# A chunked recurrence between projections: more buffers for a unit's tiles, and its score products in another pair of PSUM banks

## Chip, core and metric

One NeuronCore of a Trainium2 chip runs the whole kernel. The metric is the device time of one execution in microseconds (us). TensorE is called PE, its weight loads PEld, VectorE DVE, ScalarE ACT, GpSimd POOL and SyncE, which issues every DMA here, SP. Each engine works through its own list of instructions in the order in which they stand, and semaphores make it wait for the others.

## What is computed

Two decoder layers over 1024 tokens of 1024 channels in float32. Layer 0 mixes the tokens with a gated linear recurrence (HGRN2), layer 1 with latent attention; a causal conv gated MLP follows each. The change touches layer 0's mixer alone:

```python
q, f, i, g = jnp.split(h @ w_in, 4, axis=-1)        # 8 heads of 128
forget = lb + (1.0 - lb) * jax.nn.sigmoid(f)
key_in = 1.0 - forget
log_f = jnp.log(forget)
# per head, S_t = diag(exp(log_f_t)) S_{t-1} + k_t v_t^T ; o_t = S_t^T q_t, in chunks
o = _chunk_gated_recurrence(heads(jax.nn.silu(q)), heads(key_in), heads(i), heads(log_f))
o = _rmsnorm(o, out_norm) * jax.nn.silu(heads(g))
return o.reshape(B, S, D_MODEL) @ w_out
```

## The kernel before

Tokens are cut into two halves of 512 (`hf`), channels into 8 tiles of 128. Matrix products are made of three products of float32r parts (`hi*hi`, `hi*lo`, `lo*hi`), so that every weight tile from DRAM (`wraw`) is split into `whi` (a cast on ACT) and `wlo` (a subtraction, line 131, on POOL in the recurrence and on DVE in the output projection).

The recurrence works through 16 **units**, one for each head and half. A unit has two parts.

- `project` (lines 347 to 396): 48 matmuls of 512 columns for the forget gate and the query, into two PSUM banks with the tag `mm`, then 96 matmuls of 256 columns for value and gate, into the same two banks in turn. DVE, ACT and POOL make of them the tiles `Fg`, `K`, `q`, `Q`, `v` and `g`.
- `recur` (lines 398 to 473): the diagonal products `scores(q)`, 8 small matmuls, then six levels m = 1, 2, 4, 8, 16, 32. At each level PE makes `scores(Q)` (8 small matmuls, line 406), DVE writes them under a mask into `SD` (line 429), DVE multiplies half of `Q` by the decay of the blocks (line 417), and POOL half of `K` (line 419). The next level needs both. Then come a last product of 4 matmuls (`sc64`, line 432), the copies into `ST` on ACT (lines 436 to 438), the transposes of `K` (line 443) and their copy back on ACT (line 445), and for each of four chunks `po` (lines 451 and 453) and the update of the state, `pu` (line 456) and line 461. Then the squares of `po` on ACT (line 465), a reciprocal square root in small DVE instructions, and the scaling of `g` (line 471).

`flip` (line 475 on) transposes a unit's `g` on PE into the one `misc` bank and splits it, and `put_out` writes both parts to DRAM (`o_spill`). `out_projection` (line 309) reads all heads of a half back (`oall`), and makes 8 groups of 24 matmuls of 512 columns, each added to `x` on DVE (line 303).

The program is written as: recurrence of unit i, then projection of unit i+1, then flip of unit i. That is not the order in which it runs. The framework's scheduler fixes a list for each engine before the run; it may put an instruction earlier wherever the buffers and banks that it needs come free, and it puts the projection's matmuls between the steps of the recurrence.

So the buffers set how far a unit may run into the one before. Before the change a unit's `K`, `Q`, `v` and `Fg` have two buffers each, `SD` and `ST` one, and the block decays `tot1` to `tot32` one each. PSUM has eight banks: `mm` two, `misc` one, `wo` two, `sc` two, `o` one. All scores, `sc64`, the transposes `pT` and the four `pu` share the two `sc` banks; the two `wo` banks are used by the first projection only, and by later parts of the kernel.

Of the kernel before, what the change touches and what calls it, by code (L numbers as in the profile page):

```python
# [9 lines left out]
F32 = mybir.dt.float32  # L10
# [9 lines left out]
P = 128  # L20
D = 1024
S = 1024
HF = 512
# [7 lines left out]
LEVELS = (1, 2, 4, 8, 16, 32)  # L31
# [27 lines left out]
def trunk_kernel(ctx: ExitStack, tc: tile.TileContext, x, pos, par, gout, cst, msk, w_hin, w_hout,  # L59
# [9 lines left out]
    psg = ctx.enter_context(tc.tile_pool(name="psg", bufs=2, space=PSUM))  # L69

    def ps_mm():
        return psg.tile([P, HF], F32, tag="mm", name="ps_mm")
# [68 lines left out]
    def v3(ap, a):  # L141
        return ap.rearrange("p (a b) -> p a b", a=a)

    def acc3(ps, steps):
        n = len(steps)
        for i, (lh, ll, rh, rl) in enumerate(steps):
            pe.matmul(ps, lhsT=lh, rhs=rh, start=(i == 0), stop=False)  # L147
            pe.matmul(ps, lhsT=lh, rhs=rl, start=False, stop=False)  # L148
            pe.matmul(ps, lhsT=ll, rhs=rh, start=False, stop=(i == n - 1))  # L149
# [171 lines left out]
    def hgrn(layer, h):  # L321
        with ExitStack() as st:
            tp = st.enter_context(tc.tile_pool(name="g_t", bufs=2))
            early = st.enter_context(tc.tile_pool(name="g_e", bufs=2))
            wv = st.enter_context(tc.tile_pool(name="g_wv", bufs=1))
            ps = st.enter_context(tc.tile_pool(name="g_ps", bufs=1, space=PSUM))
# [24 lines left out]
            def project(hd, hf, bank=ps_mm):  # L351
                wf, wq, vgh, vgl = wts[hd]
                hh, hl, rb, y = h[hf]

                def proj(w):
                    p = bank()
                    acc3(p, [(w[0][:, k * P:(k + 1) * P], w[1][:, k * P:(k + 1) * P], hh[:, k, :], hl[:, k, :])
                             for k in range(KD)])
                    return p

                pf = proj(wf)
                Fg = early.tile([P, HF], F32, tag="F", name="Fg")
                K = tp.tile([P, HF], F32, tag="K", name="K")
                dve.tensor_tensor(out=Fg, in0=pf, in1=rb, op=ALU.mult)
                act.activation(out=K, in_=Fg, func=AF.Sigmoid, scale=-1.0)
                act.activation(out=Fg, in_=Fg, func=AF.Sigmoid)
                pool.tensor_scalar(out=Fg, in0=Fg, scalar1=oml[:, hd:hd + 1], scalar2=lb[:, hd:hd + 1],
                                   op0=ALU.mult, op1=ALU.add)
                pool.tensor_scalar(out=K, in0=K, scalar1=oml[:, hd:hd + 1], scalar2=0.0, op0=ALU.mult, op1=ALU.add)
                pq = proj(wq)  # L370
                q = early.tile([P, HF], F32, tag="q", name="q", bufs=1)
                Q = tp.tile([P, HF], F32, tag="Q", name="Q")
                dve.tensor_tensor(out=q, in0=pq, in1=rb, op=ALU.mult)  # L373
                act.activation(out=Q, in_=q, func=AF.Sigmoid)
                dve.tensor_tensor(out=q, in0=q, in1=Q, op=ALU.mult)
                dve.tensor_tensor(out=Q, in0=q, in1=Fg, op=ALU.mult)

                v = tp.tile([P, 4, P], F32, tag="v", name="v")
                g = tp.tile([P, 4, P], F32, tag="g", name="g", bufs=3)
                for tt in range(2):  # L380
                    pv = ps_mm()
                    for t2 in range(2):
                        t = 2 * tt + t2
                        ts_ = slice(t * P, (t + 1) * P)
                        acc3(pv[:, t2 * 256:(t2 + 1) * 256],
                             [(hh[:, k, ts_], hl[:, k, ts_], vgh[:, k, :], vgl[:, k, :]) for k in range(KD)])
                    p3 = v3(pv, 2)
                    for t2 in range(2):
                        t = 2 * tt + t2
                        yt = y[:, t:t + 1]  # L390
                        act.activation(out=v[:, t, :], in_=p3[:, t2, 0:P], func=AF.Identity, scale=yt)
                        act.activation(out=g[:, t, :], in_=p3[:, t2, P:2 * P], func=AF.Sigmoid, scale=yt)
                        dve.scalar_tensor_tensor(out=g[:, t, :], in0=p3[:, t2, P:2 * P], scalar=yt, in1=g[:, t, :],  # L393
                                                 op0=ALU.mult, op1=ALU.mult)
                pool.tensor_tensor(out=g, in0=g, in1=goutb[:, None, :].broadcast_to([P, 4, P]), op=ALU.mult)
                return Fg, K, q, Q, v, g

            def recur(hd, hf, prj, state):
                Fg, K, q, Q, v, g = prj

                def scores(qq):
                    sc = ps.tile([P, 4, 64], F32, tag="sc", name="sc", bufs=2)
                    for c in range(4):
                        for b in range(2):
                            sl = slice(c * P + b * 64, c * P + b * 64 + 64)
                            pe.matmul(sc[b * 64:b * 64 + 64, c, :], lhsT=K[:, sl], rhs=qq[:, sl], start=True, stop=True)  # L406
                    return sc

                SD = tp.tile([P, 4, 64], F32, tag="SD", name="SD", bufs=1)
                dve.tensor_tensor(out=SD, in0=scores(q), in1=fold[:, None, 0:64].broadcast_to([P, 4, 64]), op=ALU.mult)  # L410

                def scale(tot, m):
                    nb = HF // (2 * m)
                    tv = tot.rearrange("p (b two) -> p b two", two=2)
                    Qv = Q.rearrange("p (b two m) -> p b two m", two=2, m=m)
                    Kv = K.rearrange("p (b two m) -> p b two m", two=2, m=m)
                    dve.tensor_tensor(out=Qv[:, :, 1, :], in0=Qv[:, :, 1, :],  # L417
                                      in1=tv[:, :, 0:1].broadcast_to([P, nb, m]), op=ALU.mult)
                    pool.tensor_tensor(out=Kv[:, :, 0, :], in0=Kv[:, :, 0, :],
                                       in1=tv[:, :, 1:2].broadcast_to([P, nb, m]), op=ALU.mult)  # L420
                    nt = tp.tile([P, nb], F32, tag=f"tot{m}", name=f"tot{m}", bufs=2 if m == 64 else 1)
                    dve.tensor_tensor(out=nt, in0=tv[:, :, 0], in1=tv[:, :, 1], op=ALU.mult)
                    return nt

                tot = Fg
                for li, m in enumerate(LEVELS):
                    sc = scores(Q)
                    tot = scale(tot, m)
                    dve.copy_predicated(SD, masks[:, li, None, :].broadcast_to([P, 4, 64]), sc)
                sc = ps.tile([P, 4, 64], F32, tag="sc", name="sc64", bufs=2)  # L430
                for c in range(4):
                    pe.matmul(sc[0:64, c, :], lhsT=K[:, c * P:c * P + 64], rhs=Q[:, c * P + 64:(c + 1) * P],
                              start=True, stop=True)
                ST = tp.tile([P, 4, P], F32, tag="ST", name="ST", bufs=1)
                pool.memset(ST[64:P, :, 0:64], 0.0)
                act.copy(out=ST[0:64, :, 0:64], in_=SD[0:64])
                act.copy(out=ST[64:P, :, 64:P], in_=SD[64:P])
                act.copy(out=ST[0:64, :, 64:P], in_=sc[0:64])
                tot = scale(tot, 64)

                pT = ps.tile([P, 4, P], F32, tag="sc", name="pT", bufs=2)
# [7 lines left out]
                for c in range(4):  # L449
                    first = state is None  # L450
                    pe.matmul(po[:, c, :], lhsT=ST[:, c, :], rhs=v[:, c, :], start=True, stop=first)
                    if not first:
# [40 lines left out]
            goutb = wv.tile([P, P], F32, tag="goutb", name="goutb")  # L493
            nc.sync.dma_start(out=goutb, in_=gout.partition_broadcast(P))
            nc.sync.dma_start(out=cs, in_=cst)
            mstage = tp.tile([P, len(LEVELS), 64], F32, tag="ST", name="mstage", bufs=1)
            nc.sync.dma_start(out=mstage, in_=msk)
            dve.tensor_copy(out=masks, in_=mstage)
            prj = project(0, 0, ps_wo)
            h.append(norm_x(1, "mix", layer))  # L500
            states = {}
            for i, (hd, hf) in enumerate(units):
                if i:
                    put_out(*pend[:2], flip(pend[2]))
                g, states[hd] = recur(hd, hf, prj, states.get(hd))
                pend = (hd, hf, g)
                if i + 1 < len(units):
                    if units[i + 1][0] != hd:
                        weights(units[i + 1][0])
                    prj = project(*units[i + 1])  # L510
# [456 lines left out]

    h = [norm_x(0, "mix", 0)]
    h = hgrn(0, h)
    h = ffn(0, h)  # L970
    h = mla(h)
# [77 lines left out]
```

## Time and profile before

| what | value |
|---|---|
| median of 3 runs | 2585.41 us (2581.57 to 2588.17) |
| the profiled execution | 2581.05 us |
| its span, first to last instruction | 2579.2 us |
| PE busy in the span | 2483.0 us (96%) |
| DVE, ACT, POOL busy | 1698.1, 1080.6, 392.5 us |
| mean granted clock of PE | 0.987 of full speed |
| first and last score product of the recurrence | 46.5 and 615.7 us |

The span counts from the first instruction. "Idle" of an engine in a list of waits is the time in which none of its instructions ran, put down to what came last before it went on. Matmuls are pipelined: a bar of 0.28 us stands for a matmul that may be followed by the next after 0.12 us. A float32 matmul shows as two records.

### The profile page before, as it was taken

The numbers are of one execution on the slowest core, as the hardware profiler recorded it, in microseconds if no ns is written. First come the engines' busy times: TensorE is split into PE (matmuls) and PEld (weight loads), VectorE is DVE, ScalarE is ACT, GpSimd is POOL, SyncE is SP. The second block draws the span as 40 slices with busy tenths as digits, with TensorE's granted clock in tenths as the row PEclk, the third lists the DMA queues.
The fourth block names the chain that finished last, engine by engine and source line by source line (L and its number), as shares of the span: only waits on it lengthen the run. The fifth ranks groups of instructions, "written<-read, shape, count | busy, mean of one in ns | idle before, by whom it ended". The sixth has DMA issues, their size and how long they took to land.

```text
span 2579.2 us, 35799 instructions
## 1 busy us (share of the span) xinstructions
PE 2483.0 (96%) x13860; PEld 2069.2 (80%) x13860; DVE 1698.1 (66%) x3033; ACT 1080.6 (42%) x1777; POOL 392.5 (15%) x386
## 2 busy tenths in 40 slices
PE   7999999998999999999999999999999999999999
PEld 6888888876777778888888788888877787888887
DVE  8355555555788888774535777777578888875333
ACT  5322223322444444433433566656444444443322
POOL 3334445521100000000003323221000000000000
PEclk9999999999999999999999999989999999999999
DMA  3111111343433332264331000002543333226443
GB/s 138 42 50 50 50 50 66 113 144 121 154 120 111 108 112 89 90 230 155 128 126 50 17 34 33 34 26 103 200 155 120 109 110 111 91 91 220 155 170 116
DMA packets 88298, 270.18 MB, mean 105 GB/s; under 512 B 9920, under 2 KB 10304, under 8 KB 86976
## 3 DMA queue, kind: packets, MB, share of 16 engines
q1 hardware_dynamic: 88128, 267.90, 29.5%
q8 instruction: 109, 1.79, 0.3%
q14 instruction: 61, 0.50, 0.1%
HBM read 207.04 MB, written 60.82 MB: 104 GB/s over the span
## 4 chain that ended last, share of the span: by engine, by line
PE 86%; DVE 6%; ACT 3%; DMA 3%; issue 1%; SPq 0%; ACTq 0%; DVEq 0%
PE ps_mm L251 19%; PE ps_up L251 9%; PE ps_mm L147 8%; PE ps_mm L149 8%; PE ps_mm L148 7%; PE ps_up L942 7%; PE ps_mm L942 5%; PE ps_wo L942 5%; PE ps_wo L251 3%; PE sp L710 3%; PE ps_misc L942 2%; PE sc L406 2%; PE ps_misc L167 2%; DMA open_spill<-part 1%; PE ps_wo L739 1%
## 5 line engine op out<-in xcount | busy, mean ns | idle before, releaser
L128 ACT CAST whi<-wraw 128x1024 fp32r<-128x1024 f32 (+1 forms) x328 | 321.3, 993 | 579.2 <-PE ps_misc L942 236.6
L131 DVE TENSOR_TENSOR wlo<-wraw,whi 128x1024 fp32r<-128x1024 f32 (+1 forms) x298 | 337.9, 1146 | 286.3 <-ACT whi L128 285.9
L251 PE MATMUL ps_mm<-bop,whi 128*128 128x512 f32 x1536 | 477.7, 393 | 17.3 <-ACT x L888 9.5
L251 PEld LDWEIGHTS ps_mm<-bop,whi 128*128 128x128 f32 x1536 | 285.9, 188 | 89.8 <-ACT x L888 15.4
L251 PE MATMUL ps_mm<-bop,wlo 128*128 128x512 f32 x768 | 296.4, 391 | 0.9 <-DVE wlo L131 0.9
L862 DVE SCALAR_TENSOR_TENSOR x<-x,prm,x 128x1023 f32<-128x1023 f32 (+1 forms) x176 | 223.5, 1279 | 48.9 <-ACT x L859 47.9
L251 PE MATMUL ps_up<-bop,whi 128*128 128x512 f32 x704 | 220.7, 394 | 0.9 <-ACT whi L128 0.9
L251 PEld LDWEIGHTS ps_mm<-bop,wlo 128*128 128x128 f32 x768 | 144.2, 188 | 33.6 <-DVE wlo L131 2.2
L942 PE MATMUL ps_up<-ring,whi 128*128 128x512 f32 x528 | 159.9, 389 | 0.0
L251 PEld LDWEIGHTS ps_up<-bop,whi 128*128 128x128 f32 x704 | 131.8, 188 | 33.1 <-ACT whi L128 2.6
L417 DVE TENSOR_TENSOR Q<-Q,tot 128x256 f32<-128x256 f32 x96 | 65.6, 683 | 133.2 <-PE sc L406 105.3
L147 PE MATMUL ps_mm<-vgh,hh 128*128 128x256 f32 x512 | 146.0, 285 | 5.9 <-DVE q L373 5.6
L149 PE MATMUL ps_mm<-vgh,hl 128*128 128x256 f32 x512 | 145.4, 284 | 0.0
L148 PE MATMUL ps_mm<-vgl,hh 128*128 128x256 f32 x512 | 143.8, 281 | 0.0
L859 ACT ACTIVATE x<-x,prm 128x1024 f32<-128x1024 f32 x88 | 109.3, 1243 | 70.0 <-DVE x L886 48.2
L251 PE MATMUL ps_up<-bop,wlo 128*128 128x512 f32 x352 | 138.5, 394 | 0.0
L845 DVE TENSOR_TENSOR wraw<-wraw 128x512 f32<-128x512 f32 x176 | 120.8, 686 | 2.2
L147 PE MATMUL ps_mm<-hh,whi 128*128 128x512 f32 x288 | 115.7, 402 | 2.2 <-DVE g L393 1.2
L710 PE MATMUL sp<-kk,qq 128*128 128x256 f32 (+4 forms) x480 | 109.1, 363 | 8.7 <-ACT pp L725 8.5
L942 PEld LDWEIGHTS ps_up<-ring,whi 128*128 128x128 f32 x528 | 99.2, 188 | 20.7
L149 PE MATMUL ps_mm<-hh,wlo 128*128 128x512 f32 x288 | 115.5, 401 | 0.0
L888 ACT COPY x<-ps_mm 128x512 f32<-128x512 f32 x84 | 49.1, 584 | 153.0 <-PE ps_mm L251 153.0
(296 smaller groups left out, 5544.3 us busy)
## 6 DMA issues: line engine op xcount, KB each, us to landing
wraw<-in_w_up_dram SPq DMA_DIRECT2D x104, 512.0 KB, 3.7
wraw<-in_w_down_dram SPq DMA_DIRECT2D x88, 512.0 KB, 3.5
act_spill<-x SPq DMA_DIRECT2D x44, 512.0 KB, 2.6
araw<-act_spill SPq DMA_DIRECT2D x88, 256.0 KB, 3.6
wraw<-in_w_hin_dram SPq DMA_DIRECT2D x38, 512.0 KB, 3.5
oall<-o_spill SPq DMA_DIRECT2D x64, 256.0 KB, 4.6
o_spill<-oh SPq DMA_DIRECT2D x32, 256.0 KB, 2.0
o_spill<-ol SPq DMA_DIRECT2D x32, 256.0 KB, 2.2
```

What stands on the lines that cost most here:

```text
L128: act.copy(out=hi, in_=src)
L131: lo_eng.tensor_tensor(out=lo, in0=src, in1=hi.bitcast(F32), op=ALU.subtract)
L147: pe.matmul(ps, lhsT=lh, rhs=rh, start=(i == 0), stop=False)
L148: pe.matmul(ps, lhsT=lh, rhs=rl, start=False, stop=False)
L149: pe.matmul(ps, lhsT=ll, rhs=rh, start=False, stop=(i == n - 1))
L251: pe.matmul(p, lhsT=a[l][:, ks], rhs=b[:, r, k, :], start=first and k == 0 and n == 0, stop=k == KH - 1 and n == 2, skip_group_check=not f ...
L417: dve.tensor_tensor(out=Qv[:, :, 1, :], in0=Qv[:, :, 1, :], in1=tv[:, :, 0:1].broadcast_to([P, nb, m]), op=ALU.mult)
L710: pe.matmul(sp[:, 0:n], lhsT=qq[:, a, qs], rhs=kk[:, c, cl], start=(i == 0), stop=last)
L845: dve.tensor_tensor(out=o, in0=p, in1=q, op=op)
L859: act.activation(out=y, in_=u, func=AF.Identity, scale=cw(2, ff), bias=pcol("cb", layer * 44 + ff))
L862: dve.scalar_tensor_tensor(out=y[:, i:S], in0=u[:, 0:S - i], scalar=cw(2 - i, ff), in1=y[:, i:S], op0=ALU.mult, op1=ALU.add)
L942: pe.matmul(acc[d], lhsT=w[l][:, d * P:(d + 1) * P], rhs=a[:, r], start=j == 0 and n == 0, stop=j == NFF - 1 and n == 2)
```

## The change

`Fg`, `K`, `Q` and `v` get three buffers, `SD`, `ST` (with `mstage`, which shares its tag) and every `tot` two. The seven groups of score products of a unit, `scores(...)`, move from the pool's `sc` tag to the `wo` tag, two whole banks; `sc64`, `pT` and `pu` keep the two `sc` banks. No instruction is added or removed.

```diff
-                Fg = early.tile([P, HF], F32, tag="F", name="Fg")
-                K = tp.tile([P, HF], F32, tag="K", name="K")
+                Fg = early.tile([P, HF], F32, tag="F", name="Fg", bufs=3)
+                K = tp.tile([P, HF], F32, tag="K", name="K", bufs=3)
...
-                Q = tp.tile([P, HF], F32, tag="Q", name="Q")
+                Q = tp.tile([P, HF], F32, tag="Q", name="Q", bufs=3)
...
-                v = tp.tile([P, 4, P], F32, tag="v", name="v")
+                v = tp.tile([P, 4, P], F32, tag="v", name="v", bufs=3)
...
-                    sc = ps.tile([P, 4, 64], F32, tag="sc", name="sc", bufs=2)
+                    sc = psg.tile([P, 4, 64], F32, tag="wo", name="sc", padded_shape=[P, 8, 64])
...
-                SD = tp.tile([P, 4, 64], F32, tag="SD", name="SD", bufs=1)
+                SD = tp.tile([P, 4, 64], F32, tag="SD", name="SD", bufs=2)
...
-                    nt = tp.tile([P, nb], F32, tag=f"tot{m}", name=f"tot{m}", bufs=2 if m == 64 else 1)
+                    nt = tp.tile([P, nb], F32, tag=f"tot{m}", name=f"tot{m}", bufs=2)
...
-                ST = tp.tile([P, 4, P], F32, tag="ST", name="ST", bufs=1)
+                ST = tp.tile([P, 4, P], F32, tag="ST", name="ST", bufs=2)
```

The scheduler makes other lists of it. Three places follow; a number behind a name tells one tile from another of its kind.

**The end of a unit on PE**, in the middle of the recurrence: the unit whose tiles are `Q_1790`, `K_1758` and `v_1795`, and the next, `Q_2140` and `K_2108`. Before:

```order
L432 MATMUL sc64_2014<-Q_1790,K_1758 64x64 x4
L451 MATMUL po_2034<-v_1795,ST_2019 128x128 x2
L443 MATMUL pT_2028<-ident_85,K_1758 128x128 x4
L456 MATMUL pu_2038<-v_1795,K_1758 128x128
L456 MATMUL pu_2044<-v_1795,K_1758 128x128
L453 MATMUL po_2034<-state_2040,Q_1790 128x128
L451 MATMUL po_2034<-v_1795,ST_2019 128x128
```

Of the change, from the last of 10 value-and-gate matmuls that now stand behind `sc64_2014`:

```order
L149 MATMUL ps_mm_2202<-vgh_1722,hl_409 128x256
L406 MATMUL sc_2270<-q_2139,K_2108 64x64 x8
L406 MATMUL sc_2280<-Q_2140,K_2108 64x64
L451 MATMUL po_2034<-v_1795,ST_2019 128x128
L443 MATMUL pT_2028<-ident_85,K_1758 128x128 x4
L451 MATMUL po_2034<-v_1795,ST_2019 128x128
L406 MATMUL sc_2280<-Q_2140,K_2108 64x64 x7
L147 MATMUL ps_mm_2451<-hh_111,whi_2431 128x512
L148 MATMUL ps_mm_2451<-hl_112,whi_2431 128x512
```

Before, the last product, `po`, the transposes and the `pu` follow each other with nothing between. Now 10 matmuls and the next unit's first 9 score matmuls stand ahead of `po`, and 25 matmuls of 512 columns between the transposes and `pu_2038`. In units of the other half, the next unit's first score groups and 8 matmuls of 512 columns stand ahead of `po`, and 10 with a score group ahead of `pu`.

**POOL's list** over the levels of two units, where it has to split the next head's query weights (`wlo_2438`). Before:

```order
L419 TENSOR_TENSOR K_1389<-K_1389,tot2_1586 128x64x4
L395 TENSOR_TENSOR g_1796<-g_1796,goutb_226 128x512
L419 TENSOR_TENSOR K_1389<-K_1389,tot4_1600 128x32x8
L131 TENSOR_TENSOR wlo_2438<-wraw_2435,whi_2437 128x1024
L419 TENSOR_TENSOR K_1389<-K_1389,tot8_1614 128x16x16
```

Of the change:

```order
L419 TENSOR_TENSOR K_1758<-K_1758,tot1_1941 128x128x2
L131 TENSOR_TENSOR wlo_2438<-wraw_2435,whi_2437 128x1024
L369 TENSOR_SCALAR K_2108<-K_2108,lb4_200 128x512
L367 TENSOR_SCALAR Fg_2107<-Fg_2107,lb4_200,lb3_199 128x512
L435 MEMSET ST_2369 64x4x64
L419 TENSOR_TENSOR K_1758<-K_1758,tot2_1955 128x64x4
```

The split stands now between the levels 1 and 2 of a unit, with the gate work of the next projection right behind it.

**The end of the recurrence on PE**: the last matmul of the last unit (`po_6023`) and its flip (`ps_misc_6068`). Before:

```order
L453 MATMUL po_6023<-state_6042,Q_5779 128x128
L478 MATMUL ps_misc_6068<-ident_85,g_5785 128x128 x4
L167 MATMUL ps_misc_6377<-ones_90,acc_6354 128x2 x4
L147 MATMUL ps_mm_6447<-oall_6423,whi_6443 128x512
```

Of the change, from the last two of 27 output-projection matmuls that follow that `po_6023`:

```order
L148 MATMUL ps_mm_6479<-oall_6424,whi_6475 128x512
L149 MATMUL ps_mm_6479<-oall_6423,wlo_6476 128x512
L478 MATMUL ps_misc_6068<-ident_85,g_5785 128x128 x4
L167 MATMUL ps_misc_6377<-ones_90,acc_6354 128x2 x4
L147 MATMUL ps_mm_6447<-oall_6423,whi_6443 128x512
L147 MATMUL ps_mm_6479<-oall_6423,whi_6475 128x512
```

27 matmuls have moved into the place where nothing stood; flip, token sums and the rest of the two groups follow as before. The flip of the last head of the first half, which stood inside the first group of the first output projection, now stands inside the projection ahead of it.

## Rows read from the trace of the kernel before

**Rows 1.** Busy time by stretch (us, PE, PEld, DVE, ACT, POOL, clock, DMA share, GB/s).

```profile
150.00:545.00 395.00, 375.19 (x3419) 325.39 (x3418) 216.58 (x580) 118.38 (x322) 167.69 (x156) 1.00 0.19 65
545.00:660.00 115.00, 101.52 (x587) 80.19 (x586) 63.55 (x128) 33.67 (x59) 24.48 (x20) 0.94 0.38 129
```

**Rows 2.** PE's waits, 150 to 545 us: total, times, longest.

```profile
PE pu L456 <- ACT K L445: 8.8, 12, 0.7
PE ps_mm L147 <- DVE q L373: 5.4, 12, 0.7
PE po L451 <- ACT ST L438: 3.6, 8, 0.5
PE po L453 <- DVE state L461: 1.1, 5, 0.2
```

**Rows 3.** PE's waits, 545 to 660 us, the four longest.

```profile
PE ps_misc L478 <- DVE g L471: 4.5, 1, 4.5
PE ps_mm L147 <- DMA oall<-o_spill: 4.3, 2, 2.2
PE ps_misc L167 <- DVE ol L131: 1.4, 1, 1.4
PE ps_mm L147 <- DVE x L303: 1.2, 1, 1.2
```

**Rows 4.** PE in order of time at one unit's end: start, duration, instruction, idle before.

```profile
357.71 0.28 PE L148 MATMUL ps_mm<-vgl,hh 128*128 128x256 f32 x1
357.83 0.28 PE L149 MATMUL ps_mm<-vgh,hl 128*128 128x256 f32 x1
358.03 0.68 PE L432 MATMUL sc<-Q,K 128*64 128x64 f32 x8
359.17 0.71 PE L451 MATMUL po<-v,ST 128*128 128x128 f32 x4 [0.46 <-ACT ST L438]
...
361.09 0.71 PE L456 MATMUL pu<-v,K 128*128 128x128 f32 x4 [0.73 <-ACT K L445]
...
363.73 0.69 PE L406 MATMUL sc<-q,K 128*64 128x64 f32 x16
364.24 0.64 PE L406 MATMUL sc<-Q,K 128*64 128x64 f32 x16
365.54 0.39 PE L147 MATMUL ps_mm<-vgh,hh 128*128 128x256 f32 x1 [0.66 <-DVE q L373]
```

**Rows 5.** PE in order of time, a score group between matmuls of 512 columns.

```profile
600.94 0.39 PE L149 MATMUL ps_mm<-oall,wlo 128*128 128x512 f32 x1
601.16 0.39 PE L147 MATMUL ps_mm<-oall,whi 128*128 128x512 f32 x1
601.48 0.69 PE L406 MATMUL sc<-Q,K 128*64 128x64 f32 x16
...
602.43 0.39 PE L149 MATMUL ps_mm<-oall,wlo 128*128 128x512 f32 x1
```

**Rows 6.** Busy time by stretch, the two with a granted clock of half.

```profile
560.90:564.30 3.40, 3.40 (x14) 2.38 (x13) 2.67 (x4) 3.36 (x6) 0.79 (x1) 0.50 0.00 0
...
625.80:636.00 10.20, 6.46 (x19) 4.63 (x20) 5.29 (x22) 1.88 (x3) 0.00 (x0) 0.50 0.32 104
```

**Rows 7.** Groups of instructions on POOL, 150 to 545 us: busy, mean ns of one.

```profile
L419 POOL TENSOR_TENSOR K<-K,tot 128x256 f32<-128x256 f32 x70 | 56.8, 811 | 138.2 <-PE sc L406 85.9 <-PE sc L432 23.3 <-issue 17.3
...
L131 POOL TENSOR_TENSOR wlo<-wraw,whi 128x1024 fp32r<-128x1024 f32 x13 | 31.2, 2399 | 13.7 <-ACT whi L128 13.7
...
L367 POOL TENSOR_SCALAR Fg<-Fg,lb,lb 128x512 f32<-128x512 f32 x12 | 10.4, 869 | 0.8 <-ACT Fg L366 0.8
L369 POOL TENSOR_SCALAR K<-K,lb 128x512 f32<-128x512 f32 x12 | 8.2, 687 | 5.8 <-ACT K L365 5.3
```

**Rows 8.** Groups of instructions on ACT, 150 to 545 us: the cast ahead of a split.

```profile
L128 ACT CAST whi<-wraw 128x1024 fp32r<-128x1024 f32 x16 | 16.8, 1051 | 48.5 <-DMA wraw<-in_w_hin_dram 35.0 <-DMA wraw<-in_w_hout_dram 6.9 <-PE ps_mm L148 6.5
```

**Rows 9.** Groups of instructions by form on DVE, 150 to 545 us.

```profile
L422 DVE TENSOR_TENSOR tot<-tot 128x128 f32<-128x128 f32 x11 | 13.1, 1187 | 0.0
...
L422 DVE TENSOR_TENSOR tot<-Fg 128x256 f32<-128x256 f32 x12 | 5.1, 423 | 0.1
```

More of the change, by code (lines that the diff above doesn't have):

```diff
@@ L495, in hgrn @@
             nc.sync.dma_start(out=cs, in_=cst)
-            mstage = tp.tile([P, len(LEVELS), 64], F32, tag="ST", name="mstage", bufs=1)
+            mstage = tp.tile([P, len(LEVELS), 64], F32, tag="ST", name="mstage", bufs=2)
             nc.sync.dma_start(out=mstage, in_=msk)
```

## The prediction, made before the changed kernel ran

> **What bounds the kernel now.** I read the busy times by stretch first. From 150 to 545 us, where 12 units of the recurrence follow each other, PE is busy 375.2 of 395 us, and DVE and POOL are at 55% and 42% [rows 1]. So PE's own work sets the time there, and a change that removes no work can win at most PE's 19.8 us of idle time, and what those pauses cost besides. From 545 to 660 us, where the last two units run beside the output projection, 13.5 us are idle and the granted clock is 0.94 [rows 1].
>
> PE's waits say what ends the idle time. In the middle stretch they are four, 37 in number and 18.9 us in all, and all but the gate one stand in a unit's last steps: `pu` waits for the copy of the transposed `K` (8.8 us, 12 times), `po` for the copy into `ST` (3.6 us, 8 times) and for the state (1.1 us); the value matmuls wait for DVE's reading of the query bank (5.4 us, 12 times) [rows 2]. Not one is a wait for a level's products: the matmuls put between the levels hide those. PE in order of time shows why the last steps are bare: product, `po`, transposes, `pu` and the next unit's first scores follow each other with no projection matmul between [rows 4]. At the end, PE waits 4.5 us for the last unit's scaled `g`, 4.3 us in two waits for heads that return from DRAM, 1.4 us for the one `misc` bank, and 1.2 us for an addition to `x` [rows 3]; the other 2.1 us of the 13.5 are short waits of the same kinds.
>
> **The change, step by step.** It removes and adds no instruction. What counts is where the lists now put work.
>
> *The unit's last steps.* Ahead of `po` now stand 10 matmuls of 256 columns and 9 of the next unit's score matmuls: 10 x 0.12 us [rows 4] is 1.2 us, against the 0.46 us waited. Ahead of `pu` stand 25 matmuls of 512 columns, one every 0.22 us [rows 5]: 5.5 us against 0.73 waited. In the other half's units it is 10 of them and a score group, 2.7 us. Every state update has at least that between `pu` and `po`. So the 13.5 us of waits at `pu` and `po` [rows 2] go. The query wait goes too: it arose because DVE had the next unit's first scores and states ahead of reading the query bank; now some 45 value matmuls, over 5 us, stand between the query products and the matmul that takes their bank again. **Term one: 18.9 us gained.**
>
> *What a pause costs besides.* A bar of 0.28 us is followed by the next after 0.12 [rows 4], so a pause also loses the 0.16 us by which two bars would have overlapped. 37 x 0.16 = **5.9 us gained** (term two).
>
> *More changes between kinds.* A score group that follows another takes 0.51 us [rows 4]. Put between matmuls of 512 columns it takes 1.27 us from the matmul ahead to the second behind (601.16 to 602.43), less two regular steps of 0.22 and its own 0.51: 0.3 us lost for each interruption [rows 5]. By the lists, the times that scores begin after something else rise from 119 to 134. **Term three: 15 x 0.3 = 4.5 us lost.**
>
> *The end.* The flip of the first half's last head now stands in the projection ahead of the output projection, with some 45 matmuls until its head is needed; before, it stood inside the group that needed it. That takes 2.1 of the 4.3 us at `oall` [rows 3]. 27 matmuls now follow the last `po`: 27 x 0.22 = 5.9 us against 4.5 us waited for `g`. The addition to `x` that PE waited for stood on DVE behind eight normalisations, and these behind the second of two broadcast matmuls, which PE made 19 matmuls after the first; now it follows the first, 4.2 us earlier: 1.2 us. With the 2.1 us of short waits that is 9.9 us, and 1.1 us for some 7 pauses by term two. Flip, bank and return of the last head stay a chain: 1.4 + 2.2 us remain. **Term four: 11 us gained.** SP's list gains and loses nothing; one weight fetch in each head stands two to four places later, with 3 to 5 us until its split, and the last heads' writes keep their place behind the spill of `x`.
>
> *The clock.* The granted clock is half in 3.4 us after the first `oall` wait and in 10.2 us from the end of the wait for `g` on, of which PE works 6.5 [rows 6]. The first costs 1.7 us; in the second the matmuls after the heads' return take about 3.4 us where half would do, and the flip 1.25 for 0.6: 2.4 us. I keep one such stretch of 1.7 us, since two waits remain. **Term five: 2.4 us gained.**
>
> *POOL.* The place with least room: the split of the next head's query weights stands between levels 1 and 2. It may begin when the gate products end that free its buffer, 11 matmuls after the score group, 2.5 us; then the cast of 1.05 us [rows 8], the split of 2.40, and the next gate's two scalings, 0.69 and 0.87 [rows 7]; POOL is free about 8 us after the group. PE reaches level 3's scores after some 35 matmuls of 512, 10 of 256, 7 small float32 ones and the rest of a group, about 11.4 us; the scale of `K` takes 0.81 [rows 7]. That leaves 2.6 us. I charge no wait here, but a reserve of 3 us over all units for short new waits; its bounds are 0 and a return of all that terms one and two gain, 24.8 us, the nearest rows being the waits that it would restore.
>
> A rule bears on this. In DVE's chain of block decays, the product of 128x128 takes 1187 ns and the one ahead of it, of twice the size, 423 [rows 9]: something other than its size holds it, and POOL is at work beside that chain. The Trainium skill (SBUF — State Buffer, "Who interferes with whom") says that DVE and GpSimd share one pair of ports as a lock, and whoever comes second is blocked for the whole instruction of the first. The trace agrees in kind, though its rows do not name the holder. The rule speaks against the change, since two units at once put more of DVE's chain beside POOL's instructions; if it took effect at every level, the time would be that of the slower rival below, and without it that of the sum.
>
> **Sum.** 18.9 + 5.9 - 4.5 + 11 + 2.4 - 3 = 29.7 us gained. The profiled execution took 2581.05 us, 1.87 beyond its span, and 4.4 less than the median of 2585.41. On it the change gives 2551.3; on the median's scale, which I forecast, **2556 us**.
>
> **Rivals.**
>
> *The waits come back in another place* (2567 to 2577 us). Each of PE's removed waits stood for a chain on ACT and DVE whose length does not change, and the lists were made from planned times. For: all waits before were of 0.1 to 0.7 us, small against what a plan can miss. Against: the cover at each is two to seven times the wait. If half of terms one and two return, 12 us less: 2568.
>
> *No difference* (2578 to 2593). Two units may be in flight, but by the lists the next one begins only at the old one's last product, and its first scores need a `Q` that DVE and a `K` that POOL have just made. If PE stands as long at these as it stood at `po`, `pu` and the query bank, and the new interruptions cost their 4.5 us, the end alone is left, some 7 us, which is within the spread of runs. Against it: one projection lies between the making of `Q` and `K` and their use, as before, when PE never waited there.
>
> *Slower, by POOL and DVE* (about 2600). The place is level 2 of each unit: the split, or DVE blocked by it, outlasts PE's cover, as POOL has the next gate's scalings behind it and the level's `K` behind those. If it did so by one split and one scale, 2.40 + 0.81 us, in each of 14 units, 45 us would be lost against 29.7 gained: 2600. It decides from 2.1 us a unit on, that is when POOL is 4.7 us late at the place worked out above. Against it: levels never made PE wait in this stretch, with the same splits in POOL's list [rows 2].
>
> *More than forecast* (2543 to 2546): no reserve needed and no stretch at half clock.
>
> **How the numbers follow.** Forecast, 2546 to 2567: 0.68. Waits return: 0.15. No difference: 0.08. Slower: 0.05. More: 0.04. The range 2544 to 2574 holds the first, the last and two thirds of the second, 0.82. A measurement of this kernel can tell 0.3%, 7.8 us, from nothing: faster below 2577.6, 0.87; same 0.08; slower 0.05.
>
> **What would show it.** Right: from 150 us on PE's waits at `pu` and `po` are gone or under 3 us; the first output-projection matmul comes some 22 us earlier; the wait for `g` at the flip is under 1 us, while about 3.6 us remain at `misc` and `oall`; one stretch at half clock near the end instead of two. Wrong: PE waits for `K` on POOL or `Q` on DVE at the levels; the score groups make up the time in more interruptions; or the waits vanish and PE's busy time grows by as much.

## The result and the profile after

The changed kernel takes a median of 2550.89 us (2550.34 to 2551.60, 4 runs) against 2583.53 us of the kernel before in the same session (2581.57 to 2588.17, 4 runs): a ratio of 0.9871, 95% interval 0.9854 to 0.9888, or 1.3% faster. The profiled execution took 2551.60 us with a span of 2549.8, 29.4 us less than before.

Busy time by stretch (us; then PE, PEld, DVE, ACT, POOL, clock, DMA share, GB/s), the changed kernel, the two stretches of [rows 1] and its two longest at half clock ahead of 700 us:

```profile
150.00:545.00 395.00, 394.51 (x3585) 346.36 (x3586) 225.42 (x598) 126.69 (x326) 173.60 (x162) 1.00 0.23 79
545.00:660.00 115.00, 108.94 (x532) 88.63 (x532) 66.74 (x126) 39.32 (x63) 16.01 (x10) 0.97 0.41 140
51.57:65.22 13.65, 11.13 (x90) 8.97 (x89) 9.82 (x28) 2.33 (x4) 5.06 (x7) 0.50 0.00 1
601.10:607.90 6.80, 5.82 (x13) 4.18 (x14) 5.28 (x11) 3.62 (x5) 0.00 (x0) 0.50 0.25 71
```

PE is idle for 0.5 us between 150 and 545 us, where it was 19.8. Its waits from 150 to 600 us, whole, and then the one that ends at 602 us, all of the changed kernel (total, times, longest):

```profile
PE ps_misc L167 <- DVE ol L131: 1.4, 1, 1.4
PE ps_misc L478 <- DVE g L471: 0.4, 1, 0.4
...
PE ps_mm L147 <- DMA oall<-o_spill: 2.9, 1, 2.9
```

Against [rows 2, 3]: no wait at `pu`, `po` or the query bank is left. The wait of 4.5 us for the last unit's `g` is gone; the 0.4 us above are another one, at a flip at 489.7 us, in the middle stretch. Two waits at `oall` became one, and the addition to `x` is gone. PE in order of time shows a unit's end as in [rows 4], of the changed kernel:

```profile
366.96 0.63 PE L406 MATMUL sc<-Q,K 128*64 128x64 f32 x15
367.52 0.50 PE L147 MATMUL ps_mm<-hh,whi 128*128 128x512 f32 x1
...
369.25 0.40 PE L148 MATMUL ps_mm<-hl,whi 128*128 128x512 f32 x1
369.48 0.38 PE L451 MATMUL po<-v,ST 128*128 128x128 f32 x2
369.70 0.39 PE L453 MATMUL po<-state,Q 128*128 128x128 f32 x2
369.93 0.39 PE L451 MATMUL po<-v,ST 128*128 128x128 f32 x2
370.15 0.60 PE L443 MATMUL pT<-ident,K 128*128 128x128 f32 x4
370.50 0.47 PE L149 MATMUL ps_mm<-hh,wlo 128*128 128x512 f32 x1
```

The next unit's scores and 8 projection matmuls stand ahead of `po`, more go on behind the transposes, and no row carries an idle time.

**Where the 29.4 us are.** The first matmul of the FFN is a landmark that the new order can't move against the rest. It starts at 670.6 us before and 639.6 after, 31.0 us earlier. Three stretches by that landmark and by the first and last product of the attention that follows, before and then after:

```profile
670.60:1429.90 759.30, 745.81 (x3271) 606.88 (x3270) 530.78 (x684) 319.73 (x392) 35.56 (x22) 1.00 0.35 122
1429.90:1807.70 377.80, 357.38 (x2145) 312.61 (x2144) 287.63 (x844) 238.04 (x514) 98.76 (x124) 0.94 0.12 43
...
40.00:670.60 630.60, 593.16 (x4954) 506.84 (x4953) 345.15 (x866) 185.44 (x459) 240.46 (x216) 0.99 0.22 75
```

```profile
639.60:1398.90 759.30, 745.70 (x3272) 606.73 (x3271) 530.86 (x684) 319.89 (x392) 35.90 (x22) 1.00 0.35 122
1398.90:1779.50 380.60, 361.13 (x2145) 316.26 (x2144) 287.07 (x845) 238.16 (x513) 97.69 (x123) 0.93 0.12 43
...
40.00:639.60 599.60, 590.77 (x4954) 511.95 (x4953) 344.83 (x866) 192.56 (x459) 238.58 (x215) 0.98 0.23 79
```

Up to the landmark the same 4954 matmuls stand in both. PE's idle time falls from 37.4 to 8.8 us, which is 28.6 of the 31.0; its busy time falls by 2.4. The first FFN layer takes 759.3 us in both, the attention 2.8 us more (its granted clock is 0.93 instead of 0.94, its waits are no longer than before), and the rest 1.2 less: 31.0 - 2.8 + 1.2 = 29.4.

### The profile page after: what moved, and what is told of

It reads as the page before. It is cut to its first block, busy times and chain, and to the rows that moved or that the text cites. A ratio compares the mean times of both kernels' runs of the same rounds, so it can differ in the third digit from the quotient of the medians.

```text
span 2549.8 us, 35701 instructions
## 1 busy us (share of the span) xinstructions
PE 2483.9 (97%) x13860; PEld 2077.4 (81%) x13860; DVE 1697.5 (67%) x3033; ACT 1088.0 (43%) x1777; POOL 390.3 (15%) x386
## 4 chain that ended last, share of the span: by engine, by line
PE 87%; DVE 6%; ACT 3%; DMA 2%; issue 1%; SPq 0%; ACTq 0%; DVEq 0%
PE ps_mm L251 20%; PE ps_up L251 9%; PE ps_mm L147 8%; PE ps_mm L148 8%; PE ps_mm L149 8%; PE ps_up L942 7%; PE ps_mm L942 5%; PE ps_wo L942 5%; PE ps_wo L251 3%; PE sc L406 3%; PE sp L710 3%; PE ps_misc L942 2%; PE ps_misc L167 2%; PE ps_wo L739 1%; DVE hl L230 1%
## 5 line engine op out<-in xcount | busy, mean ns | idle before, releaser
L419 POOL TENSOR_TENSOR K<-K,tot 128x256 f32<-128x256 f32 x96 | 77.9, 812 | 244.7 <-PE sc L406 194.4
L148 PE MATMUL ps_mm<-hl,whi 128*128 128x512 f32 x288 | 114.7, 398 | 0.0
```

Source lines behind the costliest of these rows:

```text
L419: pool.tensor_tensor(out=Kv[:, :, 0, :], in0=Kv[:, :, 0, :], in1=tv[:, :, 1:2].broadcast_to([P, nb, m]), op=ALU.mult)
```

## Experiments

The theory: work that PE can do now stands in a unit's last steps and at the end, and covers chains on ACT and DVE whose length hasn't changed. Open was which part of the change lets it stand there, and whether POOL has the 2.6 us to spare that the prediction gave it. All ratios are against the kernel before in the same session.

### The banks alone: e1_banks_only

```
-                    sc = ps.tile([P, 4, 64], F32, tag="sc", name="sc", bufs=2)
+                    sc = psg.tile([P, 4, 64], F32, tag="wo", name="sc", padded_shape=[P, 8, 64])
```

(on the kernel before)

> The kernel before with one part of the change: the scores move to the output projection's old banks, no tile gets a buffer more. Theory 'cover': the gain is projection matmuls standing between a unit's last steps, and the scores' own banks kept them out; in this list 23 value matmuls stand ahead of po, then the next unit's scores, then 5 projection matmuls ahead of pu (5 x 0.22 = 1.1 us against 0.73 waited), and the output projection begins as early as in the changed kernel. So 2549 to 2556 us, PE waits at pu and po under 3 us between 150 and 545 us. Rival 'buffers': with one SD and one ST, and K and Q in two, the matmuls in between wait for those tiles instead: 10 us or more of waits stay and the time is 2565 to 2578.

Measured: 2554.13 us, ratio 0.9893 (0.9878 to 0.9909). PE is busy 393.66 of 395 us in the middle stretch, with no wait at `pu` or `po`. It lies in the range of the theory; one edit carries most of the gain (1.07% of 1.29%), and the rival falls. In its trace 3 to 23 projection matmuls and up to two of the next unit's score groups stand between a unit's last product and `po`, from 168 us on, where 0 or 8 matmuls and no scores stood before. Whether it counts more that the scores have banks of their own, or that the `sc` banks are left to `sc64`, `pT` and `pu`, no run separates.

### The buffers alone: e2_tiles_only and e13_third_only

```
-                    sc = psg.tile([P, 4, 64], F32, tag="wo", name="sc", padded_shape=[P, 8, 64])
+                    sc = ps.tile([P, 4, 64], F32, tag="sc", name="sc", bufs=2)
```

(e2, on the changed kernel; e13 is the kernel before with `bufs=3` at `Fg`, `K`, `Q` and `v`, nothing else)

> The changed kernel with the scores back in their own two banks, all the added buffers kept. Theory 'cover': 24 value matmuls stand ahead of po and 24 ahead of pu here too (24 x 0.12 = 2.9 us against waits of 0.3 to 0.7), so the middle stretch gains its 18 to 22 us without the banks; the output projection starts where it did before and the last unit's end is bare, so the 11 us of the end are not had: 2559 to 2567 us. Rival 'banks': without the banks nothing of the next unit can go ahead, the waits only move: 2573 to 2584.

Measured: 2619.71 us, ratio 1.0144 (1.0129 to 1.0159). Both sides missed: it is 37 us slower than before. PE's waits from 150 to 660 us in this kernel:

```profile
PE sc L406 <- POOL K L419: 14.8, 16, 1.0
PE ps_misc L478 <- DVE g L471: 12.2, 5, 4.3
PE pu L456 <- ACT K L445: 7.8, 5, 2.2
PE sc L432 <- POOL K L419: 7.2, 7, 1.1
```

PE in order of time, the same kernel, at the last levels of one unit:

```profile
368.77 0.28 PE L149 MATMUL ps_mm<-vgh,hl 128*128 128x256 f32 x1
368.98 0.68 PE L406 MATMUL sc<-Q,K 128*64 128x64 f32 x16
370.68 0.69 PE L406 MATMUL sc<-Q,K 128*64 128x64 f32 x16 [1.01 <-POOL K L419]
372.37 0.68 PE L432 MATMUL sc<-Q,K 128*64 128x64 f32 x8 [1.00 <-POOL K L419]
372.98 0.39 PE L147 MATMUL ps_mm<-vgh,hh 128*128 128x256 f32 x1
```

Three groups of scores follow each other, and PE waits a full microsecond for `K` at the second and the third. The projection matmuls that stood between them before stand ahead of `po` now (21 to 24 behind each last product in this trace, from 226 us on, where 0 or 8 stood): the waits of [rows 2] are covered, in part, with work taken from the levels. In my expectation I had counted the cover gained and not the cover lost.

> The kernel before with the third buffers of Fg, K, Q and v alone; scores stay in their own two banks, SD, ST and the sums in one buffer. Theory: the loss of e2_tiles_only comes from the third buffers alone, since they let a unit's projection be placed ahead of the old unit's last steps, and none is left between its own levels: 2610 to 2625 us with 20 us or more of waits for K on POOL, as there. Rival: the second buffers did it, then 2578 to 2590 us as before.

Measured: 2623.99 us, ratio 1.0153 (1.0131 to 1.0175), with 13.4 and 7.3 us of waits for `K` on POOL. The time lies in the range of the theory and the rival falls: the third buffers alone make the loss. Waits are only half of it. PE's busy time up to the first FFN matmul, which starts at 719.0 us here:

```profile
40.00:719.00 679.00, 615.52 (x4954) 527.58 (x4953) 352.20 (x866) 192.35 (x459) 247.43 (x216) 0.95 0.21 70
```

Against the same 4954 matmuls of the kernel before (630.60 us, 593.16 busy, clock 0.99) the 48.4 us more are 26.0 us of idle time and 22.4 of busy time, at a lower granted clock. This profiled execution was the slowest of its four.

The scores' use of the shared banks turns the loss round, as e2 against the whole change shows. In the changed kernel's trace about one to two of the next unit's score groups stand ahead of `po`, and 4 to 20 projection matmuls. That the scores spare the matmuls for the levels is what this suggests; no run tests it apart.

The Trainium skill (Perfetto Trace Analysis, "Optimization Strategy") says that a bubble which repeats on the engine that should be saturated can mean too little SBUF or PSUM for the next tile. For the banks this case agrees (e1: 18.5 us of PE's idle time gone in the middle stretch); for the third buffers in SBUF, alone, it doesn't (e13: 1.5% slower).

### The change less a part: e3_no_third and e4_no_second

```
-                K = tp.tile([P, HF], F32, tag="K", name="K", bufs=3)
+                K = tp.tile([P, HF], F32, tag="K", name="K")
...
-                ST = tp.tile([P, 4, P], F32, tag="ST", name="ST", bufs=2)
+                ST = tp.tile([P, 4, P], F32, tag="ST", name="ST", bufs=1)
```

(the first, and the same for `Fg`, `Q`, `v`, is e3; the second, and the same for `SD`, the sums and the masks' staging tile, is e4; both on the changed kernel)

> The changed kernel with Fg, K, Q and v back in two buffers each. Theory 'cover': the list has nearly the same matmuls between a unit's last steps, so 2549 to 2555 us. Rival 'buffers': a unit's projection into K and Q must wait for the unit two back to end; PE then waits for K or Q 0.5 us or more in each of 12 units, 2557 us or more.

> The changed kernel with SD, ST and the sums tot back in one buffer each. Theory 'cover': the same matmuls stand between the last steps, a unit's copy into ST comes after the po of the unit before by 20 us and more, so 2549 to 2555 us. Rival 'buffers': the copy into SD or ST waits for the unit before, and po and the levels wait with it, 2557 us or more.

Measured: e3 2545.71 us, ratio 0.9857 (0.9843 to 0.9872); e4 2549.03 us, ratio 0.9874 (0.9858 to 0.9891). In both PE is busy all 395.00 us of the middle stretch. Neither set of buffers is needed by itself once the scores share the banks, and both intervals overlap that of the whole change. But one of the two helps: e1, which has neither, took 8.4 us more than e3 and 5.1 more than e4 in the same session, and each of its runs (2551.69 to 2557.97) is slower than all of theirs (2542.76 to 2550.78). Why stays open. e4 lies in the range of the theory. e3 came out below the range of either side; that it is really ahead of the whole change isn't settled.

### The changed kernel again, and a better end: e12_after_again, e6_direct_bank, e11_no_third_direct

> The changed kernel as it is, measured again beside the next one. It tells what the 13.7 us at half clock from 51.6 us on are (3.4 to 6.8 us there in four kernels whose first stretch has the same list). If the stretch belongs to single executions: a profile with 3.4 or 6.8 us there and a span some 3 to 5 us shorter, the median 2546 to 2551. If it belongs to this kernel: 13.7 us again and 2550 to 2552.

Measured: 2550.19 us, ratio 0.9863 (0.9841 to 0.9885). Its profile has a span of 2548.5. Busy time by stretch around the same place in the head:

```profile
50.30:53.70 3.40, 3.40 (x15) 2.17 (x11) 2.31 (x11) 0.00 (x0) 1.03 (x1) 0.50 0.00 0
53.70:57.10 3.40, 1.35 (x33) 1.08 (x32) 2.41 (x9) 0.00 (x0) 1.70 (x2) 1.00 0.00 0
57.10:60.50 3.40, 3.27 (x34) 2.37 (x34) 2.42 (x6) 0.58 (x1) 0.90 (x2) 0.50 0.00 0
```

Two times 3.4 us at half clock here, 13.65 us in the first profile: with the same program and the same waits there (1.3, 1.1 and 1.1 us), the length differs from execution to execution. The first FFN matmul starts at 636.1 us, 3.5 us earlier than in the first profile, where 13.65 - 6.8 = 6.8 us more at half clock would cost 3.4 by their half (an estimate). The span is only 1.3 us shorter, so 2.2 us of that were lost later. The median lies in the ranges of both sides and decides nothing; the medians of the two sessions agree within 0.7 us.

The end still had the waits of 1.4 and 2.9 us and a stretch at half clock behind them. Two edits:

```
-            put_out(*pend[:2], flip(pend[2]))
             out_projection(0, w_hout)
...
-            out_projection(1, w_hout)
+            out_projection(1, w_hout, lambda to: flip(pend[2], to))
...
+            if own and hd == HEADS - 1:
+                own([x[:, hd, :] for x in o])
+                continue
...
+        tag = "wo" if layer == 0 and hf == 0 else "misc"
+        rb = spread_scale(hf, token_scale(hf, tag=tag)[0], dve, tag)
```

(e6 on the changed kernel, e11 on e3)

> The changed kernel with the two edits at the end alone (the last head's flip written straight into the output projection's tile, sums and broadcast of the first half's normalisation in a bank of the scores), all buffers as in the change. Theory: the waits of 1.4 and 2.9 us go, a wait of about 0.7 us and no half clock there remain: some 5 to 7 us less than the changed kernel, 2542 to 2547 us; the third buffers then account for the rest of the gain of e11_no_third_direct, 2 to 5 us. Rival: the end is given back in the MLA's waits: 2548 to 2552.

> The kernel with Fg, K, Q and v in two buffers (e3_no_third), and two edits at the end: the last head's flip writes straight into the output projection's tile instead of going out to DRAM and back, and the token sums and the broadcast of the first half's normalisation take a bank of the scores instead of the one misc bank. Theory: the 1.4 us at misc and the 2.9 us at oall go; in their place PE waits once for the copy and the subtraction that split the flipped head, about 2 us. 2 to 4 us less than e3_no_third with what the half clock gives back: 2541 to 2545. Rival: the end's time is set by DVE's normalisation, then PE waits the same 4 us at the broadcast: 2544 to 2548.

Measured: e6 2544.34 us, ratio 0.9848 (0.9822 to 0.9874); e11 **2540.85 us**, ratio 0.9825 (0.9800 to 0.9851). PE at the end, in order of time, of e11:

```profile
591.43 0.60 PE L482 MATMUL ps_misc<-ident,g 128*128 128x128 f32 x4
592.70 0.73 PE L147 MATMUL ps_mm<-oall,whi 128*128 128x512 f32 x2 [0.68 <-ACT oall L128]
593.43 0.50 PE L148 MATMUL ps_mm<-oall,whi 128*128 128x512 f32 x1
```

and its busy time from 545 us to its first FFN matmul:

```profile
545.00:628.50 83.50, 82.62 (x409) 66.99 (x408) 54.73 (x100) 29.47 (x43) 11.70 (x9) 1.00 0.38 125
```

One wait of 0.68 us is left, where I had expected about 2 in e11, and the clock is full. e11 ended 0.15 us below its range; e6 fell into its own. The first FFN matmul starts at 628.5 us in e11, 631.9 in e3; at 631.0 in e6, 636.1 in e12. Which of the two edits did how much of this isn't separated. e11 beats both kernels: its runs (2534.05 to 2543.66) all lie below those of the change in the same session (2546.10 to 2551.76). How much of its lead over e6 is the buffers' stays open, since the two ratios' intervals overlap. The intervals of e6 and of the change overlap too, so that by its time alone e6's lead isn't settled.

### POOL's room: e9_split_twice, e10_split_thrice, e8_split_on_dve

```
         split(raw, hi, lo, lo_eng=lo_eng)
+        for _ in range(again):
+            lo_eng.tensor_tensor(out=lo, in0=raw, in1=hi.bitcast(F32), op=ALU.subtract)
...
-                wq = load_w(w_hin[hd])
+                wq = load_w(w_hin[hd], again=1 if hd else 0)
```

(e9; `again=2` is e10. e8 makes the same split on DVE instead. The trace has 9 added splits in e9 and 18 in e10, not the seven and 14 of the expectations: 9 x 2.4 = 22 and 43 us.)

> The changed kernel with POOL's split of each next head's query weights made twice, with the same values: 2.4 us more on POOL in each of seven heads. Theory of the prediction: at that place POOL has 2.6 us to spare, so nothing or little comes to PE: 2546 to 2555 us, waits for K on POOL under 2 us in all. Rival 'POOL or its hold on DVE is near the bound': each costs most of its 2.4 us, 7 x 2.4 = 17 us: 2561 or more.

> The same split made three times, 4.8 us more in each of seven heads. Theory of the prediction: 2.2 us of it are more than POOL has to spare, so 7 x 2.2 = 15 us come to PE as waits for K: 2558 to 2570 us. Rival 'more room than 2.6 us': 2546 to 2555. Rival 'near the bound': 7 x 4.8 = 34 us, 2578 or more.

> The changed kernel with the split of each next head's query weights taken from POOL (2.4 us each) to DVE. Theory: DVE instructions that lie beside a POOL split are held for its length, but one such hold in a unit is hidden behind PE's matmuls: 2545 to 2553 us, within the spread of the changed kernel, with fewer DVE instructions of 2 us and more. Rival: the holds reach PE at the rate of the doubled split, a third of POOL's time, 9 x 2.4 / 3 = 7 us: 2540 to 2544.

Measured: e9 2557.55 us, ratio 0.9897 (0.9875 to 0.9919); e10 2564.91, ratio 0.9930 (0.9902 to 0.9958); e8 2551.77, ratio 0.9870 (0.9854 to 0.9886). Against 2550.19 of e12, in whose session they ran, e9 and e10 lose 7.4 and 14.7 us, a third of what POOL got. e9 hits neither range and e10's 14.7 matches the 15 of the theory, but by another mechanism: PE doesn't wait for `K` at all. Its waits from 150 to 545 us in e9:

```profile
PE po L455 <- DVE state L463: 4.2, 2, 2.1
PE ps_misc L480 <- DVE g L473: 0.7, 1, 0.7
```

They are on DVE, as all the longer ones of e10 in this stretch are (5.0 us for `state`, 4.4 for `g`, 3.0 for `Q`); in the head another one, for DVE's `acc`, grew from 1.3 us to 3.4 in e9 and 5.6 in e10. POOL and then DVE ahead of the first wait, in order of time, e9:

```profile
444.36 2.39 POOL L131 TENSOR_TENSOR wlo<-wraw,whi 128x1024 fp32r<-128x1024 f32 x1
446.71 0.93 POOL L421 TENSOR_TENSOR K<-K,tot 128x256 f32<-128x256 f32 x1
447.60 2.58 POOL L140 TENSOR_TENSOR wlo<-wraw,whi 128x1024 fp32r<-128x1024 f32 x1
```

```profile
444.43 2.61 DVE L424 TENSOR_TENSOR tot<-Fg 128x256 f32<-128x256 f32 x1 [4.18 <-POOL Fg L369]
446.96 0.97 DVE L419 TENSOR_TENSOR Q<-Q,tot 128x256 f32<-128x256 f32 x1
447.85 0.44 DVE L431 COPY_PREDICATED SD<-masks,sc 128x256 f32<-128x256 uint8 x1
448.18 2.41 DVE L424 TENSOR_TENSOR tot<-tot 128x128 f32<-128x128 f32 x2
```

A product of 128x256 that takes 423 ns alone [rows 9] starts 0.07 us behind POOL's split and lasts 2.61 us, to 0.3 us behind the split's end; two small ones beside the second split last 2.41. The predicated copy between, which reads PSUM, takes its 0.44 us in the middle of the split. This is what the Trainium skill (SBUF — State Buffer, "Who interferes with whom") says: a DVE instruction with two inputs in SBUF and a POOL instruction that reads SBUF exclude each other. These rows now show the holder, which [rows 9] left open.

In the change itself such holds stay hidden. The same product over the middle stretch (count, ns least/median/most), of the changed kernel and then of e8:

```profile
L422 DVE TENSOR_TENSOR tot<-Fg x12: 413/426/2612, 154.2 to 511.0; 128x256 f32<-128x256 f32 x12
```

```profile
L422 DVE TENSOR_TENSOR tot<-Fg x12: 417/426/427, 153.6 to 506.5; 128x256 f32<-128x256 f32 x12
```

In the changed kernel two of the twelve were held beside a split (2.61 and 2.58 us), and no wait of PE followed. With the split off POOL this product is never held, and the time is the same, as the theory had it: PE's cover takes one hold. The test is a weak one, since DVE then makes the split itself, and a split that stayed on POOL still held another of DVE's products for 2.44 us. Of the seven doubled splits of e9 in this stretch two reached PE; the other five brought no wait.

## Why the prediction was right

The predicted 2556 us (2544 to 2574) against 2550.9; by the profiled span, 29.7 us forecast and 29.4 measured. The mechanism held, but a match within 0.3 us is luck: errors of some us each, a slip in the addition among them, cancelled, and the medians (2583.53 and 2550.89) are 32.6 us apart. Point by point:

- **An addition was wrong.** The six terms of the sum add to 30.7 us, not 29.7. By its own terms the forecast should have read 2555.
- **Term one, 18.9 us of waits.** All of these are gone; with the new 0.4 us at a flip, 18.5 us were won. Right, and for the reason given, as e1 shows; which part of the change did it was left open by the prediction, and it is mostly the banks.
- **Term four, the end.** The idle time of terms one and four (18.9 + 9.9 us) was to fall by 28.8; it fell by 28.6 up to the first FFN matmul. The wait for the last unit's `g` is gone (under 1 us forecast); `misc` and `oall` cost 1.4 + 2.9 = 4.3 us where 3.6 stood in the forecast.
- **Terms two, three and five, and the reserve.** Overlap at pauses (5.9 + 1.1), interruptions (-4.5), clock (2.4) and reserve (-3) come to 1.9 us. PE's busy time for the same matmuls fell by 2.4, and by 5.7 in e12's profile. Busy time at half clock counted at half its length (an estimate: half of 3.28 + 3.40 + 6.46 us before, of 11.13 + 5.82 in the first profile, of 3.40 + 3.27 and, from 596.4 us on, 3.95 in e12) takes the clock out of it. What is left is 586.6 us before, 582.3 and 582.2 after: 4.3 and 4.4 us less, where terms two and three and the pauses at the end forecast 2.5. The reserve was not needed. Of an interruption the rows of the changed kernel give the price again:

```profile
320.00 0.28 PE L147 MATMUL ps_mm<-vgh,hh 128*128 128x256 f32 x1
320.20 0.69 PE L406 MATMUL sc<-Q,K 128*64 128x64 f32 x16
320.82 0.38 PE L148 MATMUL ps_mm<-vgl,hh 128*128 128x256 f32 x1
321.04 0.28 PE L149 MATMUL ps_mm<-vgh,hl 128*128 128x256 f32 x1
```

  1.04 us from the matmul ahead to the second behind, less 2 x 0.12 and 0.51, is 0.29 us, as charged. Terms two and three were not measured apart from each other.
- **The clock was the mis-sized term.** At the end one stretch remained, as forecast, but of 6.8 us and not 3.4. The profile's head ran 13.65 us at half clock, where the kernel before has this stretch:

```profile
55.76:59.17 3.41, 3.28 (x34) 2.38 (x34) 2.42 (x6) 0.58 (x1) 0.90 (x2) 0.50 0.00 0
```

  No step of mine had it; (13.65 - 3.41) / 2 = 5.1 us. By the estimate above the clock cost 8.5 us up to the first FFN matmul, 6.6 before: 1.9 us lost, where term five forecast 2.4 gained. With 28.6 us of idle time and 4.3 of busy time this gives the 31.0; the 1.6 us lost behind that matmul stood in no term. e12 (6.8 us there) shows that the length is not the kernel's alone, and e1 and e4 had 3.4 us there, like the kernel before; what the change does to it on average stays open.
- **POOL.** No wait for `K` came, as forecast, and of new waits only the 0.4 us for DVE's `g`; but the place was wrong. I looked for the tight spot at `K` on POOL, level 2, with 2.6 us to spare. Doubling the split there brought no wait for `K`; it brought waits on DVE for `state` and `acc`.
- **One sign failed.** The first matmul of the output projection was to come some 22 us earlier. It came 13.3 earlier (544.4 to 531.1 us), because the order had moved it: 4320 matmul records since 40 us stand ahead of it before and 4411 after. The changed kernel has done 4307 by 523.0 us, some 21 us ahead.
- **The rivals.** "Waits come back in another place" and "no difference" didn't happen with the whole change; the first is part of what e13 does, which loses 40 us. "Slower, by POOL and DVE" has a real mechanism at a third of its price: 14.7 us with 43 us more on POOL. The hold of DVE by POOL that the prediction weighed takes effect, but what it takes from DVE is hidden here.

## What to carry to other kernels

When PE is nearly full, count for every place from which a fill is taken, not only for the place that it fills: third buffers alone let the order spend its projection matmuls at the unit's end, the levels went bare, and with the lower clock that came with it the loss was 1.5%. Before giving SBUF tiles more buffers, look whether a pair of private PSUM banks is what keeps the next unit's work out; here moving one tile's tag brought 1.1% of the 1.3%. And a step's slack on POOL is to be looked for also on DVE, beside POOL's long instructions.

## What the runs showed of the hardware

- A POOL split of 2.4 us holds a DVE instruction with two SBUF inputs until it ends (423 ns became 2.61 us), and lets one that reads PSUM pass (0.44 us beside it).
- The same list with the same waits of PE in the head ran 13.65 us at half clock in one execution and 6.8 in another. By its half, the difference is worth 3.4 us (an estimate; the next landmark moved by 3.5), more than the difference between several of the kernels above; a single profile can't rank them.
